# Value pages on VectorE in two wide instructions in place of four narrow ones, and another pace for the pages

## The chip, the cores and the metric

The kernel runs on one core of one Trainium2 chip. The metric is the device time of one execution in microseconds (us); the kernel before took 1392.24 us, the median of three runs (1391.69 to 1393.86). Two runs of this kernel that differ by less than about 0.2% can't be told apart.

The engines are called by two names: TensorE (PE in the profile, PEld for its weight loads), VectorE (DVE), ScalarE (ACT), GpSimd (POOL) and SyncE (SP, whose queue issues nearly all DMAs here).

## What is computed

One layer of a hybrid decoder: 1024 prompt positions and 8 samples with one new position each, 1032 columns in all, model width 1024, everything in float32. The part that matters here is the attention of the 8 samples over their past, 1024 positions that lie in 8 pages of 128 each, found by a page table:

```python
k_past = cache_k[l][page_table].reshape(DB, -1, H_DIFF, 2, DH_DIFF)
v_past = cache_v[l][page_table].reshape(DB, -1, H_DIFF, DV_DIFF)
do = diff_attn_sample(dq, dk, dv, k_past, v_past, lam)
# in it: scores of two maps per head, softmax over past and new position,
p = jax.nn.softmax(jnp.concatenate([s_past, s_new], axis=-1), axis=-1)
a = diff_combine(p, lam)                 # p of map 0 minus lam times p of map 1
o = einsum('bhqk,bkhe->bqhe', a[..., :P], v_past) + einsum('bhqk,bkhe->bqhe', a[..., P:], dv)
```

So for each sample and page the key page (128 positions x 4 heads x 128) is multiplied by the sample's query and reduced, and later the value page (the same shape) is multiplied by one weight per position and head and summed over the pages. Around it stand the input projection, four prompt heads of differential attention, four retention heads, the output projection and a gated feed-forward part with a short convolution.

## The kernel before

**Stages.** The input projection comes first (about 10 to 520 us of the profiled execution), with all of the attention and retention in it; then the output projection and the norms (to about 700 us), the feed-forward input (to about 1100) and output. The change touches the first stage alone.

**Units.** The input projection is made of 84 units: 28 column blocks of the weights (e) times 3 segments of 344 columns (s). A unit is 24 products on TensorE (L114 to L116, ps_in) into one PSUM bank, and one VectorE instruction that scales it into z (L220), called its evacuation. Two or three banks take turns, so a product can only begin when the evacuation two or three units earlier is done. Units are counted here from zero by their L220.

**Work on the side.** After each unit the loop in `step_kernel` advances three generators by credits. `sides` runs the prompt heads one after the other, first four `diff_head` (scores L345 and L346 into sps, mask and row minimum L348, exponential L400, two maps combined by L405 to L409, transposes L292 into tp, products with the values L366 into ops, a sub-norm L304 to L307), then four `ret_head` (L617 att, L639 st, opr L686, sub-norm L304 to L307 with the power L306 on GpSimd, m L698 and L699, mtr L712). `sample_attention` is the pager: it is started after the unit of e = 19, s = 2, and advances by K_PACE steps per unit while it handles key pages and by V_PACE once it handles value pages.

**The pager.** 64 key pages, then 64 value pages, each one DMA of 256 KB into one of four buffers (pg), issued by SyncE (L462) behind a load of the page number. A key page is multiplied by the query on GpSimd (L493) and reduced by VectorE (L484, sc). After the last one come transposes (L509, st_ps), minimum (L513, mna), exponential and weights (L522 to L533, selc, L540, at). Then the value pages, two samples at a time: of each pair one sample's page goes to VectorE, the other's to GpSimd (V_POOL = (1,)), where a product L577 and a sum L579 of 128x512 each follow one another. VectorE uses one scalar_tensor_tensor of 128x128 per head (L586), or tensor_scalar for a first page (L584). After eight pages the sums go through TensorE (L558, L561, os_ps).

**What sets the order.** The text of the loop is not the order of the engines: a planner (Tile) places every instruction by its own estimates of readiness and by the order of issue, engine by engine, and each engine then runs its list in order. The paces change what is issued when, and with that the planner's lists on all engines.

Of the kernel before, what the change touches and what calls it, by code (L numbers as in the profile page):

```python
# [13 lines left out]
ALU = mybir.AluOpType  # L14
# [4 lines left out]
P = 128  # L19
# [10 lines left out]
H = 4  # L30
# [12 lines left out]
    return [(c, min(P, n - c)) for c in range(0, n, P)]  # L43


D_RATE, R_RATE, K_PACE, V_PACE = 1.42, 0.88, 3.0, 2.35
PG_BUFS, AHEAD, TAIL = 4, 2, 2
V_AHEAD, V_POOL = 3, (1,)

# [2 lines left out]
def step_kernel(ctx: ExitStack, tc: tile.TileContext, gam, g128, xT, w_in, w_o, w_f, w_y, norms, ngb, cst, subln,  # L52
                lams, rdec, alibi, alibi_s, kpool, vpool, ptab, sret, cw, cb, sconv,
                yT, yN, rsp, rss, kT, vT, cvp, cvs):
    nc = tc.nc
# [92 lines left out]
    def new_acc(pl, bufs=1, n=SEG):  # L148
        return pl.tile([P, n], F32, tag="acc", bufs=bufs, name="acc")
# [282 lines left out]
    def sample_attention():  # L432
# [41 lines left out]
        def get(ahead):  # L474
            while len(pages) < ahead + 1 and todo:
                pages.append(page(todo.pop(0)))
            return pages.pop(0)
# [64 lines left out]
        at = pk.tile([P, NPAGE, NS, H], F32, name="at")  # L542
# [10 lines left out]
        def keys_sum(b0, accs_):  # L553
            os_ps = bank("t", "os_ps")[:, 0:P]
            for h in range(H):
                o = os_ps[32 * h:32 * h + 32]
                if b0 == 0:
                    nc.tensor.matmul(o, lhsT=dx[:, 32 * h:32 * h + 32], rhs=vx, start=True, stop=False,  # L558
                                     skip_group_check=True)
                for i, acc in enumerate(accs_):  # L560
                    nc.tensor.matmul(o, lhsT=ez[:, NS - b0 - i:40 - b0 - i], rhs=acc[:, h, :],  # L561
                                     start=(b0 + i > 0 and i == 0), stop=(i == 1), skip_group_check=True)
            if b0 == 0:
                nc.scalar.activation(on_s[:, 0, :], os_ps, AF.Copy)
            else:
                nc.vector.tensor_tensor(on_s[:, 0, :], on_s[:, 0, :], os_ps, ALU.add)

        PR["v"] = True
        for b0 in range(0, NS, 2):
            accs_v = [pk.tile([P, H, P], F32, tag="qb", bufs=2, name="acc_v") for _ in range(2)]  # L570
            for p in range(NPAGE):
                for i, acc in enumerate(accs_v):
                    b = b0 + i
                    vp = get(V_AHEAD)
                    if i in V_POOL:
                        a = at[:, p, b, :].unsqueeze(2).broadcast_to([P, H, P])
                        nc.gpsimd.tensor_tensor(vp if p else acc, vp, a, ALU.mult)  # L577
                        if p:
                            nc.gpsimd.tensor_tensor(acc, acc, vp, ALU.add)  # L579
                    else:  # L580
                        for h in range(H):
                            a = at[:, p, b, h:h + 1]
                            if p == 0:
                                nc.vector.tensor_scalar(acc[:, h, :], vp[:, h, :], a, None, ALU.mult)  # L584
                            else:
                                nc.vector.scalar_tensor_tensor(acc[:, h, :], vp[:, h, :], a, acc[:, h, :],  # L586
                                                               ALU.mult, ALU.add)
                    yield
            yield
            yield  # L590
            yield
            keys_sum(b0, accs_v)
# [155 lines left out]
    for n, e in enumerate(blocks_left):  # L748
# [6 lines left out]
        for s in range(3):  # L755
            ps = bank(("mm", "mm", "S" if "pool" in PR else "mm")[s], "ps_in")[:, 0:SEG]
            z_unit(e, s, w, ps)
            if n == 0 and s == 0:
                dg = rstd_1(px, squares_x(2))
            if n == 0 and s == 1:  # L760
                x_last(dg)
                closed(px_cm)
                tail_a()
            z_evac(e, s, ps)
            if done >= 3:
                credit += D_RATE if e >= 16 else R_RATE
                while credit >= 1.0:
                    next(side, None)
                    credit -= 1.0
            if e == 19 and s == 2:  # L770
                PR["pager"] = sample_attention()
            if "pager" in PR:
                pages_due += V_PACE if "v" in PR else K_PACE
                while pages_due >= 1:
                    pages_due -= 1
                    if next(PR["pager"], 0) == 0:
                        del PR["pager"]
                        break
# [100 lines left out]
    for s in range(3):  # L879
        mh, ml = mhl[s]  # L880
        acc = new_acc(pw, 2)
# [321 lines left out]
    for part in range(2):  # L1203
# [7 lines left out]
        acc = new_acc(py, 2, YS)  # L1211
# [51 lines left out]
    for f in range(NF):  # L1263
        wh, wl, a = y_next.pop(0)
# [8 lines left out]
        if 12 <= f < 16:  # L1273
            b, c = divmod(f - 12, 2)
# [133 lines left out]
```

## Time and profile before

| | us |
|---|---|
| median of three runs | 1392.24 |
| lowest and highest run | 1391.69, 1393.86 |
| profiled execution | 1392.55 |
| its span, first to last instruction | 1390.8 |

In the profiled execution the key pages' GpSimd work starts between 160.6 and 304.3 us and the value pages' between 323.4 and 483.4. Times of rows are counted from the start of the span. Busy times of TensorE overlap in part, since its products are pipelined: a product of 344 columns is listed with some 330 ns, and the next one starts about 158 ns after it. A wait in the list of waits is idle time of an engine and what ended it.

### The profile page before, as it was taken

The page shows a single profiled execution, that of the slowest core. Times are in us where ns is not written, and L with a number is a line of the kernel's source. Part 1 is how long each engine was busy: PE and PEld are TensorE (multiplying, and loading weights), DVE is VectorE, ACT ScalarE, POOL GpSimd, SP SyncE. Part 2 cuts the span into 40 slices and gives each one's busy share as a digit, 9 for nine tenths or more (in the row PEclk, how much of TensorE's full clock was granted, in tenths as well). Part 3 has the DMA queues.
Part 4 walks back from the last instruction along what each step waited for, and adds up shares of the span by engine and source line. Part 5 has one row for each costly group of instructions (what it writes and reads, how often), then busy time and mean ns, then how long its engine had stood idle before and what let it go on. Part 6 is the DMA issues. An engine that isn't in the chain of part 4 may idle for free.

```text
span 1390.8 us, 22794 instructions
## 1 busy us (share of the span) xinstructions
PE 1316.7 (95%) x8235; PEld 1269.2 (91%) x8235; DVE 977.7 (70%) x1773; ACT 573.9 (41%) x1148; POOL 491.7 (35%) x402
## 2 busy tenths in 40 slices
PE   6999989889999999996799999999999999989998
PEld 5999887878999998996799999999999999989976
DVE  6575759879678865477877777767777655576585
ACT  5254515235222144343444434344444435546544
POOL 5300456745546621438523313323323100050130
PEclk9999999999999999998999999999999999999999
DMA  5434285764554534231122222221221268668675
GB/s 220 127 101 126 86 245 185 214 205 125 164 192 144 176 111 160 90 127 52 68 76 77 94 87 71 82 82 65 83 81 66 95 224 270 214 210 260 198 237 161
DMA packets 98355, 196.51 MB, mean 141 GB/s; under 512 B 17595, under 2 KB 47419, under 8 KB 98243
## 3 DMA queue, kind: packets, MB, share of 16 engines
q1 hardware_dynamic: 91378, 183.45, 41.6%
q10 hardware_dynamic: 6864, 11.62, 2.3%
q8 instruction: 64, 1.05, 0.3%
q14 instruction: 49, 0.39, 0.1%
HBM read 155.11 MB, written 30.48 MB: 133 GB/s over the span
## 4 chain that ended last, share of the span: by engine, by line
PE 64%; DVE 15%; POOL 7%; DMA 6%; issue 5%; ACT 2%; SPq 1%; POOLq 0%; DVEq 0%; ACTq 0%
PE ps_in L114 4%; PE ps_in L115 4%; PE ps_in L116 4%; PE ps_y L1218 3%; PE ps_y L1217 3%; PE ps_y L1219 3%; DVE acc_v L586 3%; PE pb L1023 3%; PE pb L1024 3%; PE pb L1022 3%; PE gp L1022 2%; PE up L1024 2%; PE pc L1023 2%; PE pc L1024 2%; PE up L1023 2%
## 5 line engine op out<-in xcount | busy, mean ns | idle before, releaser
L114 PE MATMUL ps_in<-xh,wh 128*128 128x344 f32 x672 | 223.6, 333 | 8.0 <-ACT xh L192 6.1
L115 PE MATMUL ps_in<-xl,wh 128*128 128x344 f32 x672 | 220.1, 328 | 2.1 <-DVE xl L193 2.1
L116 PE MATMUL ps_in<-xh,wl 128*128 128x344 f32 x672 | 218.6, 325 | 1.0 <-DVE wl L109 1.0
L114 PEld LDWEIGHTS ps_in<-xh,wh 128*128 128x128 f32 x672 | 129.0, 192 | 11.4 <-ACT xh L192 6.1
L160 POOL TENSOR_TENSOR acc<-acc,sq 128x344 f32<-128x344 f32 (+1 forms) x56 | 61.3, 1095 | 205.6 <-ACT sq L159 201.0
L115 PEld LDWEIGHTS ps_in<-xl,wh 128*128 128x128 f32 x672 | 128.9, 192 | 4.8 <-DVE xl L193 3.8
L1158 DVE TENSOR_TENSOR wyl<-wyraw,wyh 128x1024 fp32r<-128x1024 f32 x66 | 84.4, 1279 | 67.0 <-ACT wyh L1157 64.7
L116 PEld LDWEIGHTS ps_in<-xh,wl 128*128 128x128 f32 x672 | 128.9, 192 | 1.5 <-DVE wl L109 1.3
L1041 POOL TENSOR_TENSOR S<-wraw 128x512 f32<-128x512 f32 x20 | 30.8, 1541 | 266.5 <-DMA wraw<-in_w_f 239.3
L1218 PE MATMUL ps_y<-al,wyh 128*128 128x388 f32 x352 | 119.4, 339 | 2.4 <-DVE al L1169 2.4
L1219 PE MATMUL ps_y<-ah,wyl 128*128 128x388 f32 x352 | 119.1, 338 | 1.2 <-DVE wyl L1158 1.2
L1217 PE MATMUL ps_y<-ah,wyh 128*128 128x388 f32 x352 | 119.7, 340 | 0.3 <-ACT wyh L1157 0.3
L493 POOL TENSOR_TENSOR pg<-pg,qb 128x512 f32<-128x512 f32 x64 | 90.6, 1434 | 40.7 <-DMA pg<-in_kpool 26.6
L1157 ACT ACTIVATE wyh<-wyraw 128x1024 fp32r<-128x1024 f32 x66 | 69.7, 1056 | 59.5 <-PE ps_y L1218 33.1
L990 DVE TENSOR_TENSOR ww<-S,ww 128x512 fp32r<-128x512 f32 x80 | 85.4, 1086 | 8.4 <-ACT ww L989 8.4
L990 DVE TENSOR_TENSOR ww<-wraw,ww 128x512 fp32r<-128x512 f32 x80 | 74.8, 935 | 21.5 <-ACT ww L989 19.8
L989 ACT ACTIVATE ww<-wraw 128x512 fp32r<-128x512 f32 x80 | 50.2, 628 | 95.8 <-PE up L1024 65.5
L989 ACT ACTIVATE ww<-S 128x512 fp32r<-128x512 f32 x80 | 50.5, 634 | 94.1 <-POOL S L1042 35.0
L1169 DVE TENSOR_TENSOR al<-ar,ah 128x388 fp32r<-128x388 f32 (+2 forms) x110 | 62.5, 578 | 25.5 <-ACT ah L1168 24.7
L108 ACT ACTIVATE wh<-wraw 128x1024 fp32r<-128x1024 f32 (+1 forms) x41 | 42.5, 1036 | 83.3 <-PE ps_in L115 38.6
L1023 PE MATMUL pb<-tw,ww 128*128 128x344 f32 x240 | 76.8, 320 | 0.0
L1024 PE MATMUL pb<-tw,ww 128*128 128x344 f32 x240 | 76.8, 320 | 0.0
(324 smaller groups left out, 3877.6 us busy)
## 6 DMA issues: line engine op xcount, KB each, us to landing
wyraw<-in_w_y SPq DMA_DIRECT2D x66, 512.0 KB, 4.0
wraw<-in_w_f SPq DMA_DIRECT2D x44, 512.0 KB, 3.3
pg<-in_kpool SPq DMA_DIRECT2D x64, 256.0 KB, 3.0
pg<-in_vpool SPq DMA_DIRECT2D x64, 256.0 KB, 2.8
wraw<-in_w_in SPq DMA_DIRECT2D x27, 512.0 KB, 4.2
ar<-ad SPq DMA_DIRECT2D x44, 194.0 KB, 3.9
ad<-cc SPq DMA_DIRECT2D x20, 344.0 KB, 2.2
ar<-ad SPq DMA_DIRECT2D x44, 150.0 KB, 3.4
```

Of the source, the lines that this page charges most:

```text
L114: nc.tensor.matmul(ps, lhsT=wh[:, k, :], rhs=ah[:, k, n0:n1], start=(first and i == 0), stop=False)
L115: nc.tensor.matmul(ps, lhsT=wh[:, k, :], rhs=al[:, k, n0:n1], start=False, stop=False)
L116: nc.tensor.matmul(ps, lhsT=wl[:, k, :], rhs=ah[:, k, n0:n1], start=False, stop=(last and i == len(order) - 1))
L493: nc.gpsimd.tensor_tensor(kp, kp, qb.rearrange("p (a b) -> p a b", b=P), ALU.mult)
L989: nc.scalar.activation(hi, t, AF.Copy)
L990: nc.vector.tensor_tensor(lo, t, hi.bitcast(F32), ALU.subtract)
L1023: nc.tensor.matmul(ps, lhsT=w[:, 0, k], rhs=bl, start=False, stop=False, skip_group_check=True)
L1024: nc.tensor.matmul(ps, lhsT=w[:, 1, k], rhs=bh, start=False, stop=(last and k == 3), skip_group_check=True)
L1158: nc.vector.tensor_tensor(wl, raw, wh.bitcast(F32), ALU.subtract)
L1217: nc.tensor.matmul(pss[d], lhsT=wh[:, i, w], rhs=ah, start=(f == 0), stop=False)
L1218: nc.tensor.matmul(pss[d], lhsT=wh[:, i, w], rhs=al, start=False, stop=False)
L1219: nc.tensor.matmul(pss[d], lhsT=wl[:, i, w], rhs=ah, start=False, stop=(f == NF - 1))
```

## The change

Three things change. On VectorE a value page is now handled as on GpSimd: one tensor_tensor of 128x512 that multiplies the page in place by the weights, repeated along each head's 128 columns (L577), and one that adds the product to the sum (L579); for a first page one multiplication that writes the sum. K_PACE goes from 3.0 to 2.3 and V_PACE from 2.35 to 3.1.

```diff
-D_RATE, R_RATE, K_PACE, V_PACE = 1.42, 0.88, 3.0, 2.35
+D_RATE, R_RATE, K_PACE, V_PACE = 1.42, 0.88, 2.3, 3.1
...
                     vp = get(V_AHEAD)
-                    if i in V_POOL:
-                        a = at[:, p, b, :].unsqueeze(2).broadcast_to([P, H, P])
-                        nc.gpsimd.tensor_tensor(vp if p else acc, vp, a, ALU.mult)
-                        if p:
-                            nc.gpsimd.tensor_tensor(acc, acc, vp, ALU.add)
-                    else:
-                        for h in range(H):
-                            a = at[:, p, b, h:h + 1]
-                            if p == 0:
-                                nc.vector.tensor_scalar(acc[:, h, :], vp[:, h, :], a, None, ALU.mult)
-                            else:
-                                nc.vector.scalar_tensor_tensor(acc[:, h, :], vp[:, h, :], a, acc[:, h, :],
-                                                               ALU.mult, ALU.add)
+                    a = at[:, p, b, :].unsqueeze(2).broadcast_to([P, H, P])
+                    eng = nc.gpsimd if i in V_POOL else nc.vector
+                    eng.tensor_tensor(vp if p else acc, vp, a, ALU.mult)
+                    if p:
+                        eng.tensor_tensor(acc, acc, vp, ALU.add)
```

Lines below the change are 8 lower in the changed kernel (L617 is L609 there, L698 is L690). In the order, the key pages' reductions stand in units 25 to 47 before and after. The value pages on VectorE stand in 15 units before (49 to 52, 56 to 59, 64 to 66, 72 to 75) and in 19 after (54 to 58, 61 to 65, 68 to 72, 74 to 77). The copies that open the last attention head (ks, qs, kl, L324 to L331) stand between the 45th and 52nd key page load in SyncE's queue before, and together behind the 40th after; st_ps moves from units 45 to 47 to unit 52.

The first place is the end of the last attention head on VectorE, before the change (`pt`, `sps`, `cf` are of the attention head, `acc_v` and `pg` of the value pages):

```order
L348 ISA mn 128x1
L409 SCALAR_TENSOR_TENSOR pt<-pt,cf 128x896
L348 ISA pt,mn<-sps,bias 128x512
L348 ISA mn 128x1
L586 SCALAR_TENSOR_TENSOR acc_v<-pg,at,acc_v 128x128
L348 ISA pt,mn<-sps,bias,mn 128x512
L348 ISA mn 128x1
L586 SCALAR_TENSOR_TENSOR acc_v<-pg,at,acc_v 128x128 x6
L405 RECIPROCAL rs<-sm 128x2
```

and the same place after the change:

```order
L409 SCALAR_TENSOR_TENSOR pt<-pt,cf 128x896
L348 ISA pt,mn<-sps,bias 128x512
L348 ISA mn 128x1
L348 ISA pt,mn<-sps,bias,mn 128x512
L348 ISA mn 128x1
L348 ISA pt,mn<-sps,bias 128x512
L348 ISA mn 128x1
L348 ISA pt,mn<-sps,bias,mn 128x512
```

The value pages have moved out from between the head's last scores; the first one comes some 30 instructions later.

The second place is the sub-norm of the first retention head on VectorE (`ss`, `att`, `rrn`: the sub-norm; `m`: the samples' norm), before:

```order
L304 TENSOR_SCALAR ss<-ss 128x4
L307 TENSOR_TENSOR att<-att,rrn 128x512
L220 SCALAR_TENSOR_TENSOR z<-ps_in,rbc 128x344
L304 TENSOR_SCALAR ss<-ss 128x4
L307 TENSOR_TENSOR att<-att,rrn 128x512
L220 SCALAR_TENSOR_TENSOR z<-ps_in,rbc 128x344
L698 TENSOR_SCALAR m_5245<-t_5243 128x8
```

and after:

```order
L304 TENSOR_SCALAR ss<-ss 128x4
L307 TENSOR_TENSOR att<-att,rrn 128x512
L220 SCALAR_TENSOR_TENSOR z<-ps_in,rbc 128x344
L577 TENSOR_TENSOR acc_v<-pg,at 128x512
L579 TENSOR_TENSOR acc_v<-acc_v,pg 128x512
L304 TENSOR_SCALAR ss<-ss 128x4
L307 TENSOR_TENSOR att<-att,rrn 128x512
L577 TENSOR_TENSOR pg<-pg,at 128x512
L220 SCALAR_TENSOR_TENSOR z<-ps_in,rbc 128x344
L690 TENSOR_SCALAR m_5045<-t_5043 128x8
```

Page operations now stand between the two halves of the sub-norm.

The third place is GpSimd at the sub-norm of the second retention head, before:

```order
L577 TENSOR_TENSOR pg<-pg,at 128x512
L224 COPY zs<-z 128x8
L306 TENSOR_TENSOR rrn<-ss,ct 128x4 x2
L699 TENSOR_TENSOR m_5936<-m_5936,ct 128x8
L224 COPY zs<-z 128x8
```

and after:

```order
L577 TENSOR_TENSOR pg<-pg,at 128x512
L306 TENSOR_TENSOR rrn<-ss,ct 128x4
L579 TENSOR_TENSOR acc_v<-acc_v,pg 128x512
L577 TENSOR_TENSOR pg<-pg,at 128x512
L579 TENSOR_TENSOR acc_v<-acc_v,pg 128x512
L577 TENSOR_TENSOR pg<-pg,at 128x512
L579 TENSOR_TENSOR acc_v<-acc_v,pg 128x512
L306 TENSOR_TENSOR rrn<-ss,ct 128x4
```

Five page operations stand between the two powers; at the first retention head it is two.

## Rows read from the trace of the kernel before

**Rows 1.** The page: the span, and the busy times of its first part

```profile
span 1390.8 us, 22794 instructions
PE 1316.7 (95%) x8235; PEld 1269.2 (91%) x8235; DVE 977.7 (70%) x1773; ACT 573.9 (41%) x1148; POOL 491.7 (35%) x402
```

**Rows 2.** Busy time by stretch; the first line names the columns

```profile
core 0: us, PE busy (x) PEld busy (x) DVE busy (x) ACT busy (x) POOL busy (x), PEclk, DMA share, GB/s
200.00:272.00 72.00, 67.12 (x434) 62.16 (x434) 63.38 (x136) 28.97 (x71) 48.25 (x37) 1.00 0.68 208
272.00:309.00 37.00, 31.85 (x192) 28.50 (x191) 25.45 (x58) 9.74 (x23) 19.57 (x16) 1.00 0.70 195
309.00:356.00 47.00, 42.90 (x297) 39.69 (x295) 42.26 (x107) 22.74 (x53) 23.33 (x20) 1.00 0.50 155
356.00:488.00 132.00, 129.13 (x965) 125.18 (x966) 106.82 (x202) 27.02 (x67) 75.32 (x62) 0.99 0.51 164
```

**Rows 3.** TensorE's waits: us in all, times, longest; 200:309, then 309:356, then 356:488

```profile
PE sps L345 <- DVE mn L348: 2.3, 4, 1.1
PE tp L292 <- DVE pt L409: 2.3, 3, 1.8
PE sps L345 <- DMA qs<-z: 1.5, 1, 1.5
PE st_ps L509 <- DVE sc L484: 0.9, 2, 0.5
PE ops L366 <- ACT pt L357: 2.3, 2, 1.7
PE tp L292 <- DVE m L698: 0.4, 1, 0.4
```

**Rows 4.** Groups on VectorE, 310:490: busy us, mean ns, idle before

```profile
L586 DVE SCALAR_TENSOR_TENSOR acc_v<-pg,at,acc_v 128x128 f32<-128x128 f32 x112 | 71.4, 692 | 3.8 <-DMA pg<-in_vpool 3.8
L584 DVE TENSOR_SCALAR acc_v<-pg,at 128x128 f32<-128x128 f32 x16 | 10.4, 703 | 0.8 <-PE os_ps L561 0.8
```

**Rows 5.** Lines L586, L579, L577: ns min/median/max, first and last start

```profile
L586 DVE SCALAR_TENSOR_TENSOR acc_v<-pg,at,acc_v x112: 334/344/2479, 327.3 to 485.0; 128x128 f32<-128x128 f32 x112
L579 POOL TENSOR_TENSOR acc_v<-acc_v,pg x28: 1265/1289/2349, 326.0 to 483.4; 128x512 f32<-128x512 f32 x28
L577 POOL TENSOR_TENSOR pg<-pg,at x28: 1041/1124/2328, 323.4 to 482.2; 128x512 f32<-128x512 f32 x28
```

**Rows 6.** Lines L990 and L1041 of the feed-forward part, the same columns

```profile
L990 DVE TENSOR_TENSOR ww<-wraw,ww x80: 676/693/1780, 698.0 to 1101.6; 128x512 fp32r<-128x512 f32 x80
L1041 POOL TENSOR_TENSOR S<-wraw x20: 1296/1528/1882, 691.0 to 1085.1; 128x512 f32<-128x512 f32 x20
```

**Rows 7.** GpSimd, then VectorE, in order of time, 834:842: start, us

```profile
837.99 1.74 POOL L1043 TENSOR_TENSOR S<-wraw 128x512 f32<-128x512 f32 x1
836.80 1.77 DVE L990 TENSOR_TENSOR ww<-wraw,ww 128x512 fp32r<-128x512 f32 x1
```

**Rows 8.** The groups of rows 4 in the stretch 356:488 alone

```profile
L586 DVE SCALAR_TENSOR_TENSOR acc_v<-pg,at,acc_v 128x128 f32<-128x128 f32 x84 | 55.9, 719 | 3.8 <-DMA pg<-in_vpool 3.8
L584 DVE TENSOR_SCALAR acc_v<-pg,at 128x128 f32<-128x128 f32 x12 | 6.9, 628 | 0.8 <-PE os_ps L561 0.8
```

**Rows 9.** VectorE in order of time: two ends of the samples' softmax

```profile
310.41 0.75 DVE L513 CUSTOM_DVE_ANT_0 sc<-st_ps,bis,mna 128x512 f32<-128x512 f32 x1 [1.09 <-DMA bis<-in_alibi_s]
320.16 0.23 DVE L531 TENSOR_SCALAR selc<-ct,sv 128x32 f32<-128x32 f32 x1
```

**Rows 10.** Busy time in two bursts of value pages; columns as in rows 2

```profile
367.00:396.00 29.00, 28.82 (x232) 27.77 (x232) 27.41 (x54) 5.88 (x9) 18.27 (x15) 1.00 0.52 157
410.00:441.00 31.00, 28.89 (x220) 27.98 (x214) 27.98 (x54) 4.32 (x7) 19.59 (x16) 0.97 0.61 191
```

**Rows 11.** GpSimd in order of time around a retention head's sub-norm

```profile
400.45 1.02 POOL L306 TENSOR_TENSOR rrn<-ss,ct 128x4 f32<-128x4 f32 x1
402.77 1.01 POOL L306 TENSOR_TENSOR rrn<-ss,ct 128x4 f32<-128x4 f32 x1 [1.31 <-DVE ss L304]
```

## The prediction

> **What bounds the kernel now.** I read the page first: TensorE is busy for 95% of a span of 1390.8 us [rows 1]. So time can only come from the stretches where TensorE waits, and the change touches one of them: the input projection with the paged attention of the 8 samples, of which I look at 200 to 488 us. The table of stretches [rows 2] comes next. TensorE is idle there for 72.00 - 67.12 = 4.9, 37.00 - 31.85 = 5.15, 47.00 - 42.90 = 4.1 and 132.00 - 129.13 = 2.9 us, 17.0 us in all. That is about all that this change can win. VectorE is busy for 69 to 90% of these stretches, and it is the engine that TensorE waits for; the list of waits says so: from 200 to 309 the long waits end with VectorE's softmax work (mn, pt), its key reduction (sc) or a copy (qs) that stands behind page loads in SyncE's queue; in 309 to 356 with pt, which ScalarE hands on from VectorE; behind 356 there is little, among it m of the retention [rows 3].
>
> The value pages run from 323 to 485 us [rows 5]. On VectorE they are 112 scalar_tensor_tensor of 692 ns mean, 71.4 us, and 16 tensor_scalar of 703 ns, 10.4 us: 81.8 us for 32 pages, 2.56 us a page [rows 4]. The same 112 have a minimum of 334 and a median of 344 ns but a maximum of 2479 [rows 5]. So half of that time isn't work: undisturbed, a page is 4 x 344 = 1376 ns.
>
> **What holds them up.** GpSimd's page operations on 128x512 run at the same time and take 1.04 to 1.29 us undisturbed [rows 5]. In the feed-forward part the trace has the very operation that the change brings, a tensor_tensor of 128x512 with both inputs in SBUF: undisturbed 676 to 693 ns [rows 6]. Beside four GpSimd tensor_tensor in a row it takes 1.77 us, and GpSimd's then take 1.74 in place of 1.30 [rows 6, 7]. So such pairs exclude one another: VectorE's instruction waits about 1.1 us, GpSimd's about 0.44.
>
> The Trainium skill, page "SBUF — State Buffer", section "Who interferes with whom", has it stricter: a VectorE instruction with two SBUF inputs and a GpSimd instruction that reads SBUF take one shared pair of ports in turn, and the later one is blocked for the whole of the other. The trace agrees with the exclusion; of its full length it shows 0.44 of 0.69 us on GpSimd's side. By that rule the time would be that of rival 3, below.
>
> **Part 1: two instructions in place of four.** Removed: 81.8 us on VectorE. Added: 28 x 2 + 4 = 60 tensor_tensor. Undisturbed 60 x 0.692 = 41.5 us, 1.38 us a page, which is what four instructions cost undisturbed: the columns double, since product and sum are now apart, and the saved starts pay for just that. All blocked, 60 x 1.77 = 106 us, 3.54 a page. So this part by itself saves nothing unless the collisions change. I take the middle, 2.46 a page: two meetings with GpSimd a page are possible in place of four, each longer; the kernel before sits in the middle of its own range too. VectorE's sum goes from 81.8 to about 79 us. On TensorE's path that is nothing.
>
> **Part 2: where the pages stand.** The order shows what the paces do. The key pages keep their units (25 to 47 before and after), but the value pages go from 15 of the units 49 to 75 to 19 of the units 54 to 77: later, fewer per unit (32/19 = 1.7 in place of 2.1), and across the sub-norms of the retention heads, which they left alone before. Three things follow.
>
> (a) The last attention head gets VectorE to itself at its end. From 309 to 356 VectorE is busy for 42.26 of 47 us, of it 71.4 - 55.9 + 10.4 - 6.9 = 19.0 with value pages [rows 2, 4, 8], and TensorE waits 2.3 us for pt and idles 4.1 us in all [rows 3, 2]. Without the pages VectorE's load there is 23 of 47 us. I take 4.1 away. What is late next: the sample's own softmax. Its chain from mna (310.41 + 0.75) to selc (320.16 + 0.23) took 9 us among the head's instructions [rows 9]; alone, some dozen short ones, I estimate 4. In the changed order one unit of 24 products covers it, 24 x 132 / 965 = 3.3 us [rows 2]. I add 0.7 us: **-3.4 us** (-4.1 to +1).
>
> (b) The copies that open the last head now stand together in SyncE's queue behind 40 page loads, not spread over the 45th to the 54th, and the score transposes (st_ps) come five units after the last key page in place of one. The waits for qs (1.5 us) and for sc at st_ps (0.9) [rows 3] go: **-2.4 us**. The scores of the last two heads stand at unit starts, two a unit, in place of bursts of four to six inside a unit. In 200 to 309 TensorE waits 2.3 us for mn and 2.3 for pt of that work [rows 3]. VectorE's load isn't smaller there, and the last head now does three more of its eight rounds among key pages. Between 0 and the 4.6 us I take not quite half: **-2 us** (-4.6 to +2).
>
> (c) The values meet the retention heads. Two of the three bursts of before tell what a burst costs: in 367 to 396 and 410 to 441 VectorE is busy for 27.41 of 29 and 27.98 of 31 us, and TensorE idles only 0.2 and 2.1 us [rows 10]: a spare bank of PSUM covers an evacuation that is late. In the 132 us from 356 to 488 VectorE's work is 106.82 - 55.9 - 6.9 = 44.0 us without its 24 pages [rows 2, 8]; with all 32 pages at 2.46 us it is 122.7 of 132, 93%, like those bursts and more even. The bursts' price is 2.3 us for 16 pages; eight pages more are about +0.8 us where they are spread. Dearer is the sub-norm: GpSimd's two powers (L306) start at 400.45 and 402.77 with 1.31 us of idle time between them [rows 11]. TensorE's transposes behind it already wait 0.4 us for m [rows 3], so there is no slack. In the changed order two page operations stand between the powers of the first retention head, 1.04 + 1.27 = 2.3 us into a hole of 1.3, and five, about 6 us, between those of the second. The delay is 1 to 2.2 us for the first and at most 4.8 for the second; I take 1.5 + 2 = 3.5, since the evacuations in between leave TensorE a unit of work. Together **+4.3 us** (0 to +25).
>
> **Sum.** -3.4 - 2.4 - 2 + 4.3 = -3.5 us. The profiled execution took 1392.55 us (span 1390.8 and 1.75 around it), 0.3 above the median of 1392.24. 1392.55 - 3.5 - 0.3 = 1388.7.
>
> **Rivals.**
> 1. *VectorE can't keep up behind unit 54: slower.* If product and sum mostly run into GpSimd, a page costs 3 us or more. It decides from 2.54 us a page on average: 44.0 + 32 x 2.54 = 125.3 us is 95% of 132, the load of the bursts, which lasted 29 and 31 us and not 132. At 3.0 VectorE needs 140 us where TensorE's work is 129: +11, with the sub-norm's 3.5 and the gains of (a) and (b), -7.8, +6.7 us: 1399. All blocked (3.54) is 157 us, +28 and, with the same 3.5 and -7.8, about +24: 1416. For it: the mean before was 2.56 although by the median half of its instructions ran free. Against it: the pages are spread over more units, so that one engine is often done when the other starts.
> 2. *It cancels: no change.* (c) takes what (a) and (b) give, or the heads' new places only move the waits along. That is a V term of 7 to 10 us in place of 4.3, or gains of half the size: 1390 to 1395. For it: VectorE's total work hardly changes, and the order is set by a planner that moves a wait as easily as it removes one.
> 3. *No overlap at all.* GpSimd's two operations and VectorE's two one after the other are 1.04 + 1.27 + 2 x 0.69 = 3.69 us a page [rows 5, 6], 118 us for 32, so 44.0 + 118 = 162 us of VectorE where TensorE has 129: the time would be some 29 us over now, 1420. The 0.44 us of [rows 7] speak against it; 2 in 100, counted with rival 1. This is the skill's rule above taken at its word.
> 4. *The change doesn't do what it says.* The order has the 60 tensor_tensor and no L586, so this is out.
>
> **How the numbers follow.** A time within 0.2% of 1392.2, 2.8 us, can't be told from no change in a measurement of this kernel. Forecast (faster, 1381 to 1389.4): 0.40. Rival 2 (1389.4 to 1395): 0.28. Rival 1 with 3: 0.32, most of it between 1395 and 1402. The lower end is all of (a) and (b) at their best and nothing lost: -4.1 - 2.4 - 4.6 = -11.1, 1381. The upper end takes in rival 1 to 3.1 us a page, another 3 us over 1399: 1402. The forecast's own range is 1381 to 1389.
>
> **What would show it.** In the profile of the changed kernel: tensor_tensor of L577 and L579 on VectorE with a mean of about 1.2 us, 60 of them in 70 to 80 us (1.5 and more is rival 1, under 0.9 a gain that I left out); TensorE's waits for pt at the end of the last head gone; no wait for qs<-z; TensorE's transposes (L292) waiting for on or m in two of the four retention heads, 1 to 3 us each, with L306 on GpSimd late behind L577 and L579. If TensorE's idle time behind the last head stays at 3 us, (c) was too dear; if it is over 10, rival 1 holds. A sum that is right with stretches that aren't would be wrong all the same.

## The result, and the profile after

The changed kernel takes 1405.43 us (median of four runs, 1403.33 to 1411.38), and the kernel before 1391.97 in the same comparison (four runs, 1388.58 to 1393.86): a ratio of 1.0116, 95% interval 1.0075 to 1.0158. Forecast was 1388.7, with a range up to 1402: the change is slower, and the time lies outside the range. The profiled execution of after is the slowest of its four, 1411.38 us, with a span of 1408.7 where [rows 1] has 1390.8. So the profiled executions differ by 17.9 us of span where the medians differ by 13.5; the parts read from them below add up to the larger figure. In the comparisons that follow, the kernel before itself spread from 1384.24 to 1396.20 us, wider than the 0.2% named ahead of the prediction, which rested on three runs.

The stretches of [rows 2] in the profile of the changed kernel, the same columns:

```profile
200.00:272.00 72.00, 59.70 (x367) 56.02 (x367) 57.36 (x124) 26.39 (x66) 40.48 (x31) 0.93 0.62 183
272.00:309.00 37.00, 33.24 (x211) 32.30 (x209) 30.45 (x69) 14.20 (x30) 25.95 (x22) 0.97 0.64 207
309.00:356.00 47.00, 45.83 (x308) 44.04 (x307) 28.46 (x75) 24.04 (x51) 7.83 (x9) 0.99 0.30 93
356.00:488.00 132.00, 122.09 (x887) 118.42 (x887) 106.49 (x146) 28.56 (x69) 89.09 (x67) 0.96 0.52 168
```

The end of the last attention head (309 to 356) is better, as forecast: TensorE is idle for 1.2 us, not 4.1. But it is idle for 12.3 us between 200 and 272 (4.9 before) and 9.9 us between 356 and 488 (2.9 before). VectorE is no busier than before in the last stretch, 106.49 against 106.82 us of 132; GpSimd went from 75.32 to 89.09. And the granted clock of TensorE is 0.93 to 0.97 in three stretches that had 0.99 or 1.00.

TensorE's waits, as in [rows 3]: first 200 to 309, then 356 to 525.

```profile
PE sps L345 <- DVE mn L348: 10.1, 6, 4.0
PE tp L292 <- DVE pt L409: 6.0, 3, 5.1
...
PE tp L292 <- DVE m L690: 4.4, 1, 4.4
PE tb L651 <- ACT sb L645: 3.7, 1, 3.7
PE tps L590 <- DVE on_s L307: 2.7, 1, 2.7
PE ps_in L114 <- ACT att L681: 1.8, 1, 1.8
```

The waits for qs and for sc at st_ps are gone, as forecast. In their place stand a few long ones: for mn and pt of the prompt heads (4.6 us in all before, 16.1 now), and for m, sb, att and on_s while value pages run.

The value pages from 350 to 515 us, on VectorE and on GpSimd: busy us, mean ns, idle time before.

```profile
L579 DVE TENSOR_TENSOR acc_v<-acc_v,pg 128x512 f32<-128x512 f32 x28 | 34.0, 1216 | 0.5
L577 DVE TENSOR_TENSOR pg<-pg,at 128x512 f32<-128x512 f32 x28 | 33.2, 1185 | 11.8 <-DMA pg<-in_vpool 9.6 <-issue 2.2
L577 DVE TENSOR_TENSOR acc_v<-pg,at 128x512 f32<-128x512 f32 x4 | 3.2, 801 | 3.9 <-PE os_ps L561 3.5 <-ACT at L543 0.4
...
L579 POOL TENSOR_TENSOR acc_v<-acc_v,pg 128x512 f32<-128x512 f32 x28 | 46.3, 1655 | 2.0
L577 POOL TENSOR_TENSOR pg<-pg,at 128x512 f32<-128x512 f32 x28 | 35.1, 1255 | 20.7 <-DMA pg<-in_vpool 14.6 <-issue 3.7 <-DVE pg L577 2.4
L577 POOL TENSOR_TENSOR acc_v<-pg,at 128x512 f32<-128x512 f32 x4 | 5.4, 1338 | 5.4 <-PE os_ps L561 5.4
```

GpSimd in the kernel before, 310 to 490 us:

```profile
L579 POOL TENSOR_TENSOR acc_v<-acc_v,pg 128x512 f32<-128x512 f32 x28 | 38.0, 1356 | 2.1
L577 POOL TENSOR_TENSOR pg<-pg,at 128x512 f32<-128x512 f32 x28 | 35.0, 1250 | 33.9 <-DMA pg<-in_vpool 23.9 <-DVE acc_v L586 7.9 <-DVE z L220 1.8
L577 POOL TENSOR_TENSOR acc_v<-pg,at 128x512 f32<-128x512 f32 x4 | 4.9, 1228 | 6.7 <-PE os_ps L561 6.7
```

A page takes VectorE 70.4 / 32 = 2.20 us, less than the 2.46 of the forecast and the 2.56 of before. GpSimd pays: its sum L579 went from a mean of 1356 ns to 1655.

### The profile page after: what moved, and what is told of

Read it like the earlier page. It is cut to its first block, busy times and chain, and to the rows that moved or that the text cites. A ratio compares the mean times of both kernels' runs of the same rounds, so it can differ in the third digit from the quotient of the medians.

```text
span 1408.7 us, 22728 instructions
## 1 busy us (share of the span) xinstructions
PE 1325.3 (94%) x8235; PEld 1283.8 (91%) x8235; DVE 977.1 (69%) x1705; ACT 580.4 (41%) x1152; POOL 496.8 (35%) x402
## 4 chain that ended last, share of the span: by engine, by line
PE 64%; DVE 15%; POOL 8%; DMA 6%; issue 4%; ACT 2%; SPq 1%; POOLq 0%; DVEq 0%; ACTq 0%
PE ps_y L1209 4%; PE ps_y L1211 4%; PE ps_y L1210 4%; PE ps_in L114 3%; PE ps_in L115 3%; PE ps_in L116 3%; PE pb L1015 3%; PE pb L1016 3%; PE pb L1014 3%; DMA pg<-in_kpool 2%; PE gp L1014 2%; PE up L1016 2%; PE pc L1015 2%; PE pc L1016 2%; PE up L1015 2%
## 5 line engine op out<-in xcount | busy, mean ns | idle before, releaser
L114 PE MATMUL ps_in<-xh,wh 128*128 128x344 f32 x672 | 227.5, 339 | 8.2 <-ACT xh L192 6.3
L115 PE MATMUL ps_in<-xl,wh 128*128 128x344 f32 x672 | 223.0, 332 | 2.0 <-DVE xl L193 2.0
L116 PE MATMUL ps_in<-xh,wl 128*128 128x344 f32 x672 | 222.3, 331 | 1.0 <-DVE wl L109 1.0
L114 PEld LDWEIGHTS ps_in<-xh,wh 128*128 128x128 f32 x672 | 132.6, 197 | 11.3 <-ACT xh L192 6.3
L115 PEld LDWEIGHTS ps_in<-xl,wh 128*128 128x128 f32 x672 | 132.4, 197 | 4.4 <-DVE xl L193 3.7
L116 PEld LDWEIGHTS ps_in<-xh,wl 128*128 128x128 f32 x672 | 132.0, 196 | 1.5 <-DVE wl L109 1.3
L982 DVE TENSOR_TENSOR ww<-S,ww 128x512 fp32r<-128x512 f32 x80 | 86.8, 1103 | 6.3 <-ACT ww L981 6.3
L220 DVE SCALAR_TENSOR_TENSOR z<-ps_in,rbc 128x344 f32<-128x344 f32 x84 | 42.5, 510 | 50.1 <-PE ps_in L116 50.0
```

The source lines that it names most:

```text
L114: nc.tensor.matmul(ps, lhsT=wh[:, k, :], rhs=ah[:, k, n0:n1], start=(first and i == 0), stop=False)
L115: nc.tensor.matmul(ps, lhsT=wh[:, k, :], rhs=al[:, k, n0:n1], start=False, stop=False)
L116: nc.tensor.matmul(ps, lhsT=wl[:, k, :], rhs=ah[:, k, n0:n1], start=False, stop=(last and i == len(order) - 1))
L982: nc.vector.tensor_tensor(lo, t, hi.bitcast(F32), ALU.subtract)
```

## Where the 18 us are

A unit's end is taken here as the start of its last product (L116) in the trace. Counted from unit 24, just before the first key page, the kernels below need this long up to unit 53 (key pages and the last two attention heads), from there to unit 83 (value pages and retention heads), and behind it. The executions differ by up to 4 us before unit 24, where their order is the same, so that part is left out. In the table "wide" is the two instructions of the change and "narrow" the four of before, the two numbers are K_PACE and V_PACE, and the last three columns are us of one profiled execution each.

| kernel | ratio of times, 95% | units 25 to 53 | 54 to 83 | behind |
|---|---|---|---|---|
| before | | 196.5 | 163.8 | 872.5 |
| after | 1.0116 (1.0075 to 1.0158) | 196.4 | 178.8 | 873.8 |
| form: wide, 3.0 and 2.35 | 1.0047 (1.0027 to 1.0066) | 196.4 | 166.7 | 870.0 |
| paces: narrow, 2.3 and 3.1 | 1.0085 (1.0055 to 1.0116) | 191.2 | 180.8 | 870.7 |
| form_v: wide, 3.0 and 3.1 | 1.0131 (1.0111 to 1.0152) | 195.5 | 184.9 | 870.2 |
| form_k: wide, 2.3 and 2.35 | 1.0126 (1.01 to 1.0152) | 192.5 | 168.6 | 885.1 |
| cross | 1.0019 (1.0004 to 1.0034) | 196.6 | 165.8 | 871.2 |
| cross_ctl | 1.0002 (0.9988 to 1.0016) | 194.9 | 165.5 | 870.1 |
| all_dve: form, no value page on GpSimd | 0.9932 (0.9912 to 0.9952) | 193.8 | 157.3 | 871.3 |
| narrow_dve: before, none on GpSimd | 0.994 (0.9918 to 0.9963) | 193.8 | 157.2 | 871.8 |
| after_dve: after, none on GpSimd | 0.9955 (0.9932 to 0.9978) | 190.8 | 160.6 | 873.9 |
| dve_2_6: all_dve with 3.0 and 2.6 | 0.9933 (0.9916 to 0.9951) | 192.5 | 156.9 | 873.9 |

So after loses its time behind unit 53: 15.0 of the 17.9 us of span. Up to unit 53 it comes out even in this execution; paces, form_k and after_dve have the same pace for the key pages and are 4 to 6 us ahead there.

The columns hide one shift. With K_PACE 2.3 the 24 small products at the end of the samples' softmax (L540, L546) stand behind unit 53 and not ahead of it; in the kernel before they hold TensorE for about 2.2 us (320.96 to 323.11). With the same work on both sides, paces, form_k and after_dve are 2 to 3 us ahead of the kernel before up to unit 53, after is 2 us behind it, and the loss of after behind unit 53 is 12.8 us.

## What one wait looks like

The largest single loss behind unit 53 is in units 71 and 72, at the second retention head. VectorE in order of time, start and duration, from the first half of the sub-norm on:

```profile
450.63 1.00 DVE L304 TENSOR_SCALAR ss<-ss 128x4 f32<-128x4 f32 x1
451.55 0.68 DVE L579 TENSOR_TENSOR acc_v<-acc_v,pg 128x512 f32<-128x512 f32 x1
453.14 1.77 DVE L307 TENSOR_TENSOR att<-att,rrn 128x512 f32<-128x512 f32 x1 [0.91 <-POOL rrn L306]
...
455.26 1.10 DVE L577 TENSOR_TENSOR pg<-pg,at 128x512 f32<-128x512 f32 x1
456.39 1.66 DVE L579 TENSOR_TENSOR acc_v<-acc_v,pg 128x512 f32<-128x512 f32 x1
457.98 1.52 DVE L577 TENSOR_TENSOR pg<-pg,at 128x512 f32<-128x512 f32 x1
459.54 1.66 DVE L579 TENSOR_TENSOR acc_v<-acc_v,pg 128x512 f32<-128x512 f32 x1
461.12 0.16 DVE L304 TENSOR_SCALAR ss<-ss 128x4 f32<-128x4 f32 x1
462.41 1.52 DVE L307 TENSOR_TENSOR att<-att,rrn 128x512 f32<-128x512 f32 x1 [1.13 <-POOL rrn L306]
463.86 1.74 DVE L577 TENSOR_TENSOR pg<-pg,at 128x512 f32<-128x512 f32 x1
465.63 0.69 DVE L579 TENSOR_TENSOR acc_v<-acc_v,pg 128x512 f32<-128x512 f32 x1
...
466.67 0.15 DVE L690 TENSOR_SCALAR m<-t 128x8 f32<-128x8 f32 x1
```

and GpSimd beside it:

```profile
457.47 1.49 POOL L577 TENSOR_TENSOR pg<-pg,at 128x512 f32<-128x512 f32 x1
459.04 1.61 POOL L579 TENSOR_TENSOR acc_v<-acc_v,pg 128x512 f32<-128x512 f32 x1
461.35 1.02 POOL L306 TENSOR_TENSOR rrn<-ss,ct 128x4 f32<-128x4 f32 x1 [0.71 <-DVE ss L304]
```

The two engines step in turn, one instruction each in 1.57 us (457.47 to 459.04 on GpSimd, 457.98 to 459.54 on VectorE): a page each in 3.14 us. The instructions of VectorE that belong to the sub-norm are caught too, L304 at 1.00 in place of 0.15, L307 at 1.77 and 1.52 in place of 0.69. The second half's L304 is late behind the pages, L307 behind that, then one more page, and m at 466.67. That is 16.0 us from the first L304 to m, with seven page instructions in between; in the kernel before it is 7.2 (444.87 to 452.02), with none. The transposes (L292), next on TensorE, have waited 4.44 us for it. GpSimd itself is prompt: its power starts 0.07 us after L304's end.

In the key pages' stretch the long waits have the same form. VectorE, which stands in order, waits for a key page with the softmax of a head behind it, or has the next head's preparation (L322, L323) put between a head's L405 and L409:

```profile
220.51 0.69 DVE L484 TENSOR_REDUCE sc<-pg 128x8 f32<-128x512 f32 x1 [3.35 <-POOL pg L493]
...
251.09 2.28 DVE L322 TENSOR_TENSOR z<-z,qs 128x1024 fp32r<-128x1024 f32 x1
...
254.42 1.21 DVE L323 TENSOR_TENSOR kl<-z,ks 128x1024 fp32r<-128x1024 f32 x1
255.56 2.28 DVE L409 SCALAR_TENSOR_TENSOR pt<-pt,cf 128x1024 f32<-128x1024 f32 x1
```

Behind each of seven waits from 200 us on (1.8 to 5.1 us) TensorE is slow in part of the next 4 to 5 us. Two of the seven stretches (behind the waits of 4.0 and 4.4 us), the columns of [rows 2]:

```profile
224.70:229.00 4.30, 4.30 (x18) 4.30 (x19) 3.82 (x11) 3.08 (x12) 2.53 (x4) 0.60 0.78 240
...
467.00:472.00 5.00, 5.00 (x24) 5.00 (x25) 4.43 (x8) 1.33 (x2) 4.25 (x3) 0.66 0.82 265
```

The granted clock is 0.60 to 0.70 in all seven (34.6 us in sum, mean 0.67): part of the time at the lower of the two levels, 1.2 GHz, which shows as 0.5, the rest at 2.4. That is some 34.6 x 0.33 = 11.5 us of TensorE's time. The kernel before has two such places between units 24 and 83, behind a wait of 2.0 us for pt at 171.6 and one of 2.1 us for st at 438.5:

```profile
171.60:177.00 5.40, 5.40 (x30) 5.13 (x31) 2.71 (x5) 1.08 (x2) 2.21 (x2) 0.68 0.43 140
437.00:446.00 9.00, 7.46 (x42) 7.47 (x43) 7.74 (x22) 2.92 (x10) 5.15 (x4) 0.81 0.51 152
```

By the same sum they cost 5.4 x 0.32 + 9.0 x 0.19 = 3.4 us. The change therefore added some 8 us of slow products.

## The experiments

**Theories.** Theory 1: the paces moved work to worse places (pages between the halves of a sub-norm, scores packed among key pages), and the form of the instructions costs nothing. Theory 2: the wide form costs, since product and sum are held up by GpSimd. The four combinations of form and paces are to tell them apart.

**form**: after with `K_PACE, V_PACE = 3.0, 2.35`.

> Two wide instructions a value page on VectorE, with the paces of the kernel before (3.0 and 2.35). Its order is that of the kernel before, instruction for instruction, only that each group of four L586 is one product and one sum. Theory 1 (the paces moved work to worse places; the form costs nothing): 1386 to 1394 us, and between 200 and 309 us no wait of TensorE over 3 us. Theory 2 (the form costs, since product and sum are held up by GpSimd): 1400 to 1408, with VectorE's page over 2.6 us and TensorE idle for more than 10 us between 309 and 488.

Ratio 1.0047. The truth is between: there is no wait over 3 us in the key pages' stretch, a page costs VectorE 69.4 / 32 = 2.17 us, and the stretch behind unit 53 is 2.9 us longer than before. The form is a small loss by itself, smaller than theory 2 has it and not the zero of theory 1. Where the rest of the 0.47% is lost, these rows don't show.

**paces**: before with `K_PACE, V_PACE = 2.3, 3.1`.

> Paces 2.3 and 3.1 with the four narrow instructions a page of the kernel before. Theory 1: 1400 to 1409 us, with the long waits of the changed kernel (L345 for mn, L292 for pt, 4 to 5 us each between 200 and 309 us) at the same places. Theory 2: 1388 to 1395.

Ratio 1.0085, 1403.4 us. As theory 1 has it, with the long waits where after has them (mn 3.4, pt 4.6 us up to 309). The longest from 356 to 540 us is L292's for m, 5.4 us.

**form_v and form_k**: after with one of the old paces back, `3.0, 3.1` and `2.3, 2.35`.

> Wide instructions, V_PACE 3.1 but K_PACE 3.0, so the key pages stand as before and the value pages in 18 units from 49 to 69. Theory 1, with both stretches to blame (key pages +9 us by the ends of units 24 to 47, value pages the rest): 1392 to 1398, the waits over 3 us between 200 and 309 gone, one at a retention head left. Theory 2: 1398 to 1406, as the pages and their collisions are all still there.

> Wide instructions, K_PACE 2.3 but V_PACE 2.35, so the key pages stand as in the changed kernel and the value pages in units 54 to 83, over all four retention heads. Theory 1: the 9 us of the key pages are lost here as in the changed kernel, 1400 to 1408, with the waits over 3 us between 200 and 309 us at the same places. Theory 2: 1398 to 1406 as well, but without more loss up to 309 us than the key pages of the kernel before have.

Both theories failed on form_v: 1.0131, the slowest, although the waits of the key pages' stretch are gone. Its values take 184.9 us; in one place TensorE waits 9.8 us for ScalarE's att, because pages on VectorE and GpSimd stand in the first half of a sub-norm (L304 ran at 467.21, its last input was there at 458.4). form_k has the new pace for the key pages, whose units 25 to 53 take 4 us less than before (2 of them by the small products that moved), and values in four bursts that keep clear of the sub-norms, 168.6 us. It loses elsewhere: the last burst runs from unit 80 on, and the output projection waits 5.9 us for mh (L778). Its 1407.4 us lie in theory 1's range, but the 9 us that this theory put into the key pages aren't lost there.

So with half of the value pages on GpSimd their place decides. Where they keep clear of the sub-norms, units 54 to 83 take 164 to 169 us; where they don't, 179 to 185.

**holes**: is the slow clock due to the waits? (Theory 3: to the page loads or the neighbours' work.) Before, with `for _ in range(n): nc.vector.tensor_copy(w[1], w[1])` behind four units.

> The kernel before, with waits made on purpose in a stretch where TensorE never waits: behind the 13th, 16th, 19th and 22nd unit VectorE copies that unit's weights (wl, 128x1024) onto themselves 1, 2, 4 and 6 times, and the next unit's products need them. Theory 1 (a wait of TensorE costs more than its length, since the granted clock falls behind it): behind the two long waits (some 4 us and more) the products stand 0.29 us apart in place of 0.158 for 3 to 5 us, 1.5 to 2.5 us lost each, and behind a wait of about 1 us they don't. Theory 3 (the slow products behind the waits of the changed kernel have to do with the page loads or with VectorE and GpSimd at work): no slow products here, since no page is loaded yet.

The planner found room for two of the four, so two waits arose, of 1.5 and, with a 2.8 us wait just before it, 8.9 us, the latter later than planned and among page loads. Behind the short one, in 167 to 171, the granted clock is 1.00; behind the long one:

```profile
196.65 0.65 PE L116 MATMUL ps_in<-xh,wl 128*128 128x344 f32 x1 [8.94 <-DVE wl L764]
197.10 0.49 PE L114 MATMUL ps_in<-xh,wh 128*128 128x344 f32 x1
197.39 0.49 PE L115 MATMUL ps_in<-xl,wh 128*128 128x344 f32 x1
```

The products start 0.29 us apart for 5.3 us, and then from one product to the next 0.16 apart: 18 x 0.13 = 2.3 us lost on top of the wait, as in after. But the granted clock was at 0.50 already from 185 to 188, in the wait of 2.8 us for an evacuation, before the 8.9 us began, and pages were loading. So this run, a single one, doesn't settle theory 3. The kernel before does for pages and GpSimd. Its last value page was issued at about 478 us and GpSimd is idle from 521.7 on, and behind a wait of 2.0 us at 527.9 the clock falls all the same:

```profile
527.88 0.40 PE L659 MATMUL tb<-ct,sb 128*128 128x128 f32 x1 [2.01 <-ACT sb L653]
```

The stretch behind it, the columns of [rows 2]:

```profile
527.90:532.00 4.10, 4.10 (x25) 3.65 (x26) 3.94 (x10) 1.06 (x1) 0.00 (x0) 0.58 0.23 77
```

So neither page loads nor GpSimd's work are needed. VectorE is at work here too (3.94 of 4.10 us); that it plays no part is not shown.

**cross and cross_ctl**: what does work between the halves of a sub-norm cost by itself? Theory 4: not the place, but collisions with GpSimd's pages. Before, with eight harmless instructions more for the second retention head, in cross behind the first half's L307:

```diff
+            [nc.vector.tensor_tensor(on[:, 0:4, :], on[:, 0:4, :], on[:, 0:4, :], ALU.max) for _ in range(8 if (h, g) == (1, 0) else 0)]
```

and in cross_ctl the same on s0, behind L703.

> The kernel before, with eight tensor_tensor of 128x512 more on VectorE (they change no value), between the two halves of the second retention head's sub-norm, where no page stands. GpSimd has no more to do. Undisturbed they take 8 x 0.69 = 5.5 us, about what the page work between the halves took in the changed kernel. Theory 1 (page work that VectorE has between the halves of a sub-norm is what costs): the transposes behind it (L292) wait 4 to 5 us for m, the products behind the wait are slow, together +5 to +9 us: 1395 to 1400. Theory 4 (not the place, but collisions of VectorE with GpSimd's pages cost): under +2 us.

> The same eight instructions in the kernel before, right behind the same sub-norm and m (from L703 on), before the next head's page burst. Theory 1: nobody on TensorE waits for them, under +2 us: 1390 to 1393. If VectorE's load in this stretch were the cause, the same as with the eight between the halves, +5 to +9.

cross is 1.0019, cross_ctl 1.0002. Theory 1 missed: eight instructions between the halves cost 2.6 us (0.6 to 4.7) and not 5 to 9. Theory 4's "under 2" lies inside that interval, but isn't shown by it either. VectorE in cross (the added ones are listed as L690), in order of time:

```profile
447.36 0.17 DVE L304 TENSOR_SCALAR ss<-ss 128x4 f32<-128x4 f32 x1
...
451.14 3.59 DVE L690 TENSOR_TENSOR att<-att 128x512 f32<-128x512 f32 x5
...
457.39 0.16 DVE L698 TENSOR_SCALAR m<-t 128x8 f32<-128x8 f32 x1
```

They take 0.71 us each; GpSimd has no page here. From the first L304 to m it is 10.0 us, 2.8 more than before, as part of the 5.7 us falls into time in which VectorE waited for the second half's squares (2.42 us before); TensorE doesn't wait for m at all. In after it is 16.0 us with seven page instructions in it.

**all_dve**: form with `V_POOL = ()`, all 64 value pages on VectorE.

> Wide instructions, the paces of the kernel before, and all 64 value pages on VectorE, none on GpSimd: no collisions. Undisturbed a page is 1.38 us, 88 us in all, where VectorE has 82 in the kernel before and 69 with the wide form and GpSimd beside it. Theory 2 (collisions are what the wide form costs): 1385 to 1392, the means of L577 and L579 at 0.7 us. Theory 1: the planner spreads the 64 pages over the units 49 to 77, four of the sub-norms' halves get page work between them, and that costs 5 us and more each: 1396 to 1410.

Ratio 0.9932, 1381.85 us: faster than both kernels, and below the ranges of both theories (theory 2 had 1385 to 1392). VectorE's page instructions and its stretch 356 to 488:

```profile
L577 DVE TENSOR_TENSOR pg<-pg,at 128x512 f32<-128x512 f32 x56 | 40.4, 739 | 3.2 <-DMA pg<-in_vpool 3.2
L579 DVE TENSOR_TENSOR acc_v<-acc_v,pg 128x512 f32<-128x512 f32 x56 | 38.9, 710 | 0.0
...
L577 DVE TENSOR_TENSOR acc_v<-pg,at 128x512 f32<-128x512 f32 x8 | 5.2, 687 | 0.9 <-PE os_ps L561 0.8
...
356.00:488.00 132.00, 132.00 (x1004) 128.81 (x1004) 107.76 (x214) 31.54 (x85) 30.48 (x19) 1.00 0.51 167
```

64 pages take VectorE 84.5 us, 1.32 a page; with the same instructions and half of the pages on GpSimd (form), 32 pages took it 69.4. So giving half of them away spares VectorE 15.1 us, and costs GpSimd 87.7. TensorE is busy for the whole of 356 to 488, although page instructions stand at the sub-norms in units 60, 61 and 69. That speaks against theory 1 as it stood, and gives theory 5: a crossing costs because GpSimd's pages stretch what VectorE has in it.

**after_dve, narrow_dve, dve_2_6**: `V_POOL = ()` in after, in before, and in all_dve with `V_PACE` 2.6.

> The changed kernel (paces 2.3 and 3.1) with all 64 value pages on VectorE, none on GpSimd. The pages stand in 24 of the units 54 to 79 and between the halves of the sub-norms at units 61 and 69 to 70, so the crossings are all there, only the collisions are gone. Theory 5 (a crossing costs only because GpSimd's pages stretch what VectorE has between the halves): the units 53 to 83 take 157 to 162 us, as with all pages on VectorE and the old paces, no wait for m over 1 us, and what is left over that kernel is the key pages' stretch, -2 to +6 us: 1380 to 1390. Theory 1 (the place of the pages is what costs): the units 53 to 83 take 170 us and more, 1395 to 1405.

> The kernel before (four narrow instructions a page, paces 3.0 and 2.35) with all 64 value pages on VectorE. Theory 5: what counts is that GpSimd is silent, the form of the page doesn't: L586 at 0.34 to 0.36 us, 1.4 a page as with the wide form, 1380 to 1386. If the wide form has a gain of its own, 1388 or more here.

> All 64 value pages on VectorE in wide instructions, K_PACE 3.0, V_PACE 2.6: the pages end in unit 75 instead of 77 and none stands between the halves of the sub-norm at unit 69. Theory 5: crossings cost nothing without GpSimd's pages, so the same as with 2.35, 1379 to 1385. Theory 1: 2 to 5 us less, since a crossing is gone.

All three times lie where theory 5 has them. after_dve is the changed kernel with its paces, 1384.5 us in place of 1405.43; behind unit 53 it takes 160.6 us, not 178.8. The planner's lists aren't those of after, but the crossings are all there and more: at the second retention head ten page instructions stand between the first L304 and m, not seven. Without GpSimd's pages that takes 10.2 us, not 16.0, and TensorE doesn't wait for m:

```profile
436.37 0.17 DVE L304 TENSOR_SCALAR ss<-ss 128x4 f32<-128x4 f32 x1
...
446.57 0.15 DVE L690 TENSOR_SCALAR m<-t 128x8 f32<-128x8 f32 x1
```

Its stretch from 356 to 488, the columns of [rows 2]:

```profile
356.00:488.00 132.00, 132.00 (x1006) 129.31 (x1005) 118.73 (x230) 30.46 (x80) 25.88 (x18) 1.00 0.58 189
```

VectorE is busier than in after, 118.73 against 106.49 us of 132, and TensorE is busy throughout. Of the waits of after from 356 on two are left, and smaller: for sb 1.5 us and for on_s 1.1.

narrow_dve shows that the form doesn't matter once GpSimd is silent (157.2 us behind unit 53, as all_dve):

```profile
L586 DVE SCALAR_TENSOR_TENSOR acc_v<-pg,at,acc_v 128x128 f32<-128x128 f32 x224 | 67.9, 359 | 0.0
L584 DVE TENSOR_SCALAR acc_v<-pg,at 128x128 f32<-128x128 f32 x32 | 6.7, 282 | 0.9 <-PE os_ps L561 0.8
```

dve_2_6 gains nothing on all_dve, but it doesn't test theory 1: its trace hasn't one crossing fewer. At the first two retention heads eight page instructions stand between the first L304 and m in each of the two kernels (7 and 1 in all_dve, 3 and 5 in dve_2_6).

## Why the prediction was wrong

**(a), the last head clear of value pages: right.** TensorE's idle time in its stretch fell by 2.9 us, against 3.4. VectorE is at 28.46 of 47 us there, against a forecast of 23.

**(b), copies and scores: half right.** The waits for qs and sc went, 2.4 us. But the scores at unit starts didn't save 2 us: the waits for mn and pt grew by 11.5 us in the profiled execution. The forecast looked at where the scores stand on TensorE, and not at what stands in front of their softmax on VectorE: a reduction that waits 3.35 us for its page, and 3.5 us of the next head's preparation ahead of L409. With the small products counted where they stood before, units 25 to 53 came out 2 us worse in after and 2 to 3 us better in three kernels with the same pace. So -7.8 for (a) and (b) was too much, and the sign held in three of four executions.

**(c), values meet the retention heads: the step that failed.** +4.3 forecast, +15.0 measured in units 54 to 83, 2.2 of them small products that moved there: 12.8. The place was right (the second retention head's sub-norm), and so was the count of page operations; three things in the term weren't. The delay was sized by GpSimd between its two powers, with undisturbed durations of 1.04 and 1.27 us; it arose on VectorE, between the second half's squares and m, from instructions of 1.5 to 1.8 us, the sub-norm's own among them. Only sub-norms were priced; sb, att and on_s came late too, at 3.7, 1.8 and 2.7 us of wait. And a wait was priced at its length. Behind each the granted clock was 0.60 to 0.70 for 4 to 5 us, about 1.6 us more for each of the seven. No term of the sum had that, although [rows 10] showed it: the granted clock of the second burst is 0.97, not 1.00.

**The page's cost: right in size, wrong in meaning.** 2.20 us a page lies between the bounds of 1.38 and 3.54, below the 2.46 taken. But "on TensorE's path that is nothing" missed who pays. Of VectorE's 11.4 us 8.9 came back on GpSimd, where L577 and L579 went from 77.9 us to 86.8. By the medians GpSimd's pages cost 21 us with these paces (after against after_dve) and 14 with the old ones (form against all_dve). How much of that is collisions, and how much the other order that the planner makes without those pages, no run separates.

**The rivals.** Rival 1 had the right sign for a wrong reason: its point of decision, 2.54 us a page, wasn't reached, and VectorE was busy for 81% of its stretch. What failed was latency at a few places, not throughput: with 90% in the same stretch after_dve is faster. TensorE's idle time from 356 to 488, 9.9 us, came to the edge of the 10 at which the prediction would have seen this rival hold. Rival 2, no change, lies outside the measured interval. Rival 3, no overlap at all, is nearer to the truth than its 2 in 100, for a place: a page on each engine takes 3.14 us where both run, 3.69 with no overlap, and 2.31 if GpSimd's alone set it. The Trainium skill, page "SBUF — State Buffer", section "Who interferes with whom", has that a VectorE instruction with two SBUF inputs and a GpSimd instruction that reads SBUF exclude one another; the rows at 454 to 461 us agree for 85% of it (3.14 of 3.69 us). The prediction named that rule and priced VectorE's instructions by rows, but didn't ask what follows for the split: VectorE alone does two pages in 2 x 1.32 = 2.64 us (all_dve).

What stays open: how much of the key pages' waits in after is chance. The same pace of key pages took 190.8 to 196.4 us for units 25 to 53 in four kernels, one execution each, and no run told why.

## What to carry to other kernels

Before a form or a pace is tuned, ask whether two engines that share the work slow one another down: compare the sum of both with the faster engine alone, here 3.14 us for two pages on two engines against 2.64 on one. Price a moved piece of work by what it delays in the chain that TensorE waits for next, with the durations that it has beside its neighbours. And price a long wait of TensorE above its length, with the slow products behind it read from the trace.

## What the hardware showed that was not expected

With the narrow form, half of the pages on GpSimd saved VectorE nothing: 81.8 us for 32 pages with GpSimd at work, 74.6 for all 64 without it (narrow_dve). Instructions of 128x128 in a row overlap: 224 of 359 ns fill 67.9 us, not 80.4, so the narrow form is even the cheaper one alone, 1.17 us a page against 1.32. And behind waits of 1.8 to 8.9 us TensorE's products stood 0.29 us apart for some 2 to 5 us and then, from one to the next, 0.16; behind one of 1.5 us (holes, at 166) and one of 1.8 us (after, for pt at 173) they didn't, nor behind one of 2.7 us (before, at 682, granted clock 1.00). The wait for pt at 171.6 in the kernel before, 2.0 us, did bring them. So the wait's length alone doesn't tell.
